# One float32 row loaded by two queues instead of one, in a batched trace of matrix products

## The chip, the core and the metric

The kernel runs on one NeuronCore of a Trainium2 chip. A core has a matrix engine (PE, with its weight loads listed apart as PEld), a vector engine (DVE), a scalar engine (ACT), a general engine (POOL) and a synchronising engine (SP). Sixteen DMA engines move data between the large memory (HBM) and the core's on-chip memory of 128 partitions. The metric is the device time of one execution in microseconds (us).

## The reference

```python
def setup_inputs():
    B, N = 8, 2176
    return {"a": np.random.randn(B, N, N).astype(np.float32),
            "b": np.random.randn(B, N, N).astype(np.float32)}

def reference(a, b):
    prod = np.matmul(a, b)
    return np.diagonal(prod, axis1=1, axis2=2).sum(axis=-1).astype(np.float32)
```

For each of eight pairs the result is the trace of A times B, which is the sum over all i and k of A[i, k] times B[k, i]. Nothing but the elementwise product of A transposed with B has to be formed, so the kernel reads 16 matrices of 2176 x 2176 float32 (303 MB) and does little arithmetic on each number.

## The kernel before

A matrix has 17 blocks of 128 rows. They are held as three groups: two of six blocks (the tiles `a_six` and `b_six` hold both, twelve blocks) and one of five (the tile `five`). Within a group of m blocks, partition p holds the m neighbouring rows m\*p to m\*p+m-1, so that each partition reads one contiguous stretch of HBM. All of these tiles are bfloat16, and the loads of them are issued by POOL (`fetch`, line 178); these loads convert from float32 on the way. They all go through one queue, called q0 on the page, and are carried out in the order of issue.

For every pair n the steps are: PE transposes blocks of A into PSUM (lines 241 and 244), ACT and DVE copy the transposed blocks into the tile `at` (lines 283 and 307), and DVE multiplies `at` with B and sums the products (line 296). A pair starts with the group of five; then follow the two groups of six. The tile `five` is shared by A and B: it is filled with A's last five blocks, transposed, and filled with B's last five blocks as soon as PE has read it (POOL waits for the semaphore `made`). For the last pair, B comes in nine pieces, of which the last ones are small, and PE forms a part of the products as 128 x 128 matmuls (line 270). Two of the small loads there have 8 partitions and one has 112, and they lie in `five` too.

The first pair is loaded in a way of its own. Of A's group of five, block 0 (the first row of each partition's five) comes by a load that ACT issues (line 153). It brings 128 partitions of 2176 float32, 8,704 bytes each, with no conversion, into `words`, which is the memory of the first two blocks of `b_six` seen as float32. ACT casts the left half of it into `five[:, 0]` (line 154), DVE the right half (line 155). Blocks 1 to 4 come by POOL's first `fetch`, and `a_six` by its second. All of that stands ahead of the hand-synchronised section (`tile_critical`) or at its beginning. On entry to the section every engine but POOL waits for the two casts. POOL issues its first two fetches before it does that (`tc.wait_critical_data_deps()`).

Then DVE writes `ones` and zeros two tiles (line 293), POOL turns these into identities (line 201), and PE starts once the identities are there and SP has seen the first fetch land (line 226: SP counts the arrivals and passes them on to PE).

SP has no loads before the change. Its one DMA is the store of the eight results at the end (line 352).

Of the kernel before, what the change touches and what calls it, by code (L numbers as in the profile page):

```python
# [21 lines left out]
def kernel(  # L22
# [6 lines left out]
    nc = tc.nc  # L29
    P = 128  # L30
# [3 lines left out]
    SIX, FIVE = 6, 5  # L34
    TWICE = 2 * SIX
# [74 lines left out]
    def flat(t):  # L110
        return t.rearrange("p r k -> p (r k)")
# [4 lines left out]
    def rows_of(src, start, m, r0, r1):  # L116
        return src[start:start + P * m, :].rearrange("(p r) k -> p (r k)", r=m)[:, r0 * N:r1 * N]
# [4 lines left out]
    def last_b(v):  # L122
        if v < TWICE:
            return b_six[:, v, :]
        return five[:, v - TWICE, :]
# [24 lines left out]


    words, middle = flat(b_six[:, 0:2, :].bitcast(f32)), N // 2
    nc.scalar.dma_start(out=words, in_=rows_of(a[0], TWICE * P, FIVE, 0, 1))
    nc.scalar.copy(out=five[:, 0, :middle], in_=words[:, :middle])
    nc.vector.tensor_copy(out=five[:, 0, middle:], in_=words[:, middle:])  # L155

    with tc.tile_critical(no_gpsimd_drain=True) as section:
# [24 lines left out]
        for n in range(BATCH):  # L182
# [14 lines left out]
            if n == 0:  # L197
                tc.wait_critical_data_deps()
                gp.wait_ge(zeros.sem, 2)
                for t in (identity32, identity16):  # L200
                    ready.by(gp.affine_select(
                        out=t, in_=t, compare_op=mybir.AluOpType.not_equal, fill=1.0, base=0,
# [49 lines left out]
        for k, (piece, (lo, hi, more)) in enumerate(zip(pieces, shares)):  # L252
            mine = []
            for v in range(piece.v0, piece.v1):
                row = last_b(v)
# [45 lines left out]
        for n in range(BATCH):  # L301
# [21 lines left out]
            out=result[:1, 0:LAST],  # L323
            in_=total[:, 0:2 * LAST].rearrange("o (b n) -> o b n", n=2),
# [18 lines left out]
        for c in range(cols):  # L343
# [9 lines left out]
            out=out.rearrange("(a b) -> a b", a=1), in_=result[:1, :],  # L353
# [40 lines left out]
```

## Time and profile before

| what | value |
|---|---|
| median of 3 runs | 707.49 us (707.47 to 707.51) |
| the profiled execution's own time | 707.37 us |
| its span, first to last instruction | 705.6 us |
| POOL's loads, queue q0 | 150.96 MB written on chip, 99.8% of 16 engines' span |
| ACT's load, queue q10 | 1.11 MB in 144 packets, 0.5% |
| HBM read | 303.04 MB, 429 GB/s over the span |
| DVE, PE, ACT, POOL busy | 54%, 28%, 29%, 4% |

The 1.8 us between the span and the execution's time lie before the first instruction or after the last one. A share of a DMA queue is the time that its packets took, summed and set against 16 engines for the whole span. The trace keeps a record of each packet with its start, its length and its queue. For a load of 128 partitions there is one data packet for each partition and a 4-byte one on each of the 16 engines that reports that it is done; so the 144 packets of q10 are 128 and 16.

### The profile page before, as it was taken

What the parts mean: (1) busy time and instruction counts of PE and PEld (TensorE: products, weight loads), DVE (VectorE), ACT (ScalarE), POOL (GpSimd) and SP (SyncE); (2) the same over time, 40 slices, a digit from 0 to 9 for tenths busy, and PEclk for the clock granted to TensorE, in tenths of its full rate; (3) what the DMA queues carried; (4) which work ended last, traced back from release to release, by engine and by line L of the source; (5) the groups of instructions that cost most, each with busy time, mean ns of one, the idle gap of its engine ahead of it and who ended that gap; (6) DMA issues with size and microseconds to landing.
All of it is one profiled execution on the core that took longest, in us unless ns stands there. A gap on an engine that the chain in (4) does not pass through costs nothing. (4 is left out here: it accounts for less than half of the span.)

```text
span 705.6 us, 3919 instructions
## 1 busy us (share of the span) xinstructions
PE 200.1 (28%) x1611; PEld 180.0 (26%) x1613; DVE 381.1 (54%) x94; ACT 204.5 (29%) x162; POOL 26.1 (4%) x48
## 2 busy tenths in 40 slices
PE   0335003450134501344012440134301343014606
PEld 0224002440124401243012430124301343014504
DVE  0105488154871549715397163961639616395478
ACT  1427002470023700346003460044500445005800
POOL 1000000000000000000000000000000000002000
PEclk9759555695557955678555785567755578556957
DMA  9999999999999999999999999999999999999998
GB/s 237 213 216 208 229 207 215 216 225 213 223 220 212 211 221 216 215 214 226 209 218 227 211 210 225 215 213 214 228 206 217 226 211 214 224 217 213 215 212 160
DMA packets 7751, 152.14 MB, mean 216 GB/s; under 512 B 706, under 2 KB 962, under 8 KB 1346
## 3 DMA queue, kind: packets, MB, share of 16 engines
q0 software_dynamic: 7600, 150.96, 99.8%
q10 hardware_dynamic: 144, 1.11, 0.5%
q8 instruction: 2, 0.03, 0.0%
q14 instruction: 3, 0.02, 0.0%
q1 hardware_dynamic: 2, 0.00, 0.0%
HBM read 303.04 MB, written 0.00 MB: 429 GB/s over the span
## 5 line engine op out<-in xcount | busy, mean ns | idle before, releaser
L283 ACT COPY at<-aT 128x1536 bf16<-128x1536 bf16 (+3 forms) x160 | 202.1, 1362 | 460.0 <-DVE sums L296 357.5
L296 DVE CUSTOM_DVE_ANT_0 at<-at,b_six 128x26112 bf16<-128x26112 bf16 (+2 forms) x9 | 214.4, 23832 | 88.8 <-DMA b_six<-in_b_dram 88.8
L307 DVE COPY at<-aT 128x1536 bf16<-128x1536 bf16 (+1 forms) x48 | 80.1, 1668 | 209.3 <-PE aT L241 158.2
L241 PE MATMUL aT<-identity,five 128*128 128x128 f32 x240 | 54.0, 412 | 369.6 <-PEq L238 369.6
L241 PEld LDWEIGHTS aT<-identity,five 128*128 128x128 f32 x240 | 46.2, 220 | 375.7 <-issue 375.7
L241 PE MATMUL aT<-identity,a_six 128*128 128x128 f32 x576 | 88.4, 313 | 99.0 <-PEq L238 98.9
L241 PEld LDWEIGHTS aT<-identity,a_six 128*128 128x128 f32 x576 | 81.2, 204 | 105.4 <-issue 105.4
L296 DVE CUSTOM_DVE_ANT_0 at<-at,five 128x10880 bf16<-128x10880 bf16 (+3 forms) x10 | 84.9, 8504 | 15.2 <-ACT at L283 14.3
L244 PE MATMUL aT<-identity,a_six 128*128 128x128 bf16 x480 | 33.5, 219 | 11.0 <-PEq L238 10.9
L244 PEld LDWEIGHTS aT<-identity,a_six 128*128 128x128 bf16 x480 | 29.5, 118 | 14.4 <-issue 14.4
L178 POOL DMA_DIRECT2D five<-in_b_dram x15 | 8.2, 553 | 290.1 <-PE aT L244 290.1
L244 PE MATMUL aT<-identity,five 128*128 128x128 bf16 x200 | 15.9, 249 | 0.0
L244 PEld LDWEIGHTS aT<-identity,five 128*128 128x128 bf16 x200 | 15.7, 128 | 0.5
L178 POOL DMA_DIRECT2D five<-in_a_dram x8 | 4.6, 577 | 294.5 <-DVE sums L296 293.7
L270 PE MATMUL trace_ps<-b_six,at 128*128 128x128 bf16 x34 | 3.8, 310 | 22.1 <-DMA b_six<-in_b_dram 22.1
L270 PEld LDWEIGHTS trace_ps<-b_six,at 128*128 128x128 bf16 x34 | 3.5, 145 | 22.2 <-issue 22.2
L178 POOL DMA_DIRECT2D b_six<-in_b_dram x10 | 6.6, 663 | 37.7 <-DVE sums L296 37.7
L178 POOL DMA_DIRECT2D a_six<-in_a_dram x9 | 6.1, 680 | 0.0
L272 PE MATMUL aT<-at 128*128 128x512 bf16 x13 | 4.1, 453 | 0.3 <-issue 0.2
L270 PE MATMUL trace_ps<-five,at 128*128 128x128 bf16 x54 | 3.8, 220 | 1.3 <-DMA five<-in_b_dram 1.3
L155 DVE CAST five<-b_six 128x1088 bf16<-128x1088 f32 x1 | 0.7, 727 | 5.8 <-DMA b_six<-in_a_dram 5.8
L270 PEld LDWEIGHTS trace_ps<-five,at 128*128 128x128 bf16 x54 | 3.1, 98 | 2.8 <-DMA five<-in_b_dram 2.4
(19 smaller groups left out, 8.7 us busy)
## 6 DMA issues: line engine op xcount, KB each, us to landing
a_six<-in_a_dram POOLq DMA_DIRECT2D x7, 6528.0 KB, 54.7
b_six<-in_b_dram POOLq DMA_DIRECT2D x7, 6528.0 KB, 52.3
five<-in_b_dram POOLq DMA_DIRECT2D x7, 2720.0 KB, 22.0
five<-in_a_dram POOLq DMA_DIRECT2D x7, 2720.0 KB, 24.4
a_six<-in_a_dram POOLq DMA_DIRECT2D x2, 3264.0 KB, 46.8
b_six<-in_b_dram POOLq DMA_DIRECT2D x1, 3264.0 KB, 31.4
five<-in_a_dram POOLq DMA_DIRECT2D x1, 2176.0 KB, 14.8
b_six<-in_b_dram POOLq DMA_DIRECT2D x1, 2176.0 KB, 41.2
```

The lines of the kernel that those rows point to most:

```text
L155: nc.vector.tensor_copy(out=five[:, 0, middle:], in_=words[:, middle:])
L178: reached = count.by(gp.dma_start(out=dst, in_=src), 16)
L241: last = pe.transpose(ps[:, place, :], src, identity32)
L244: last = pe.transpose(ps16[:, place * P:(place + 1) * P], src, identity16)
L270: ins = pe.matmul(trace_ps, x, y, start=w is real[0], stop=w is real[-1])
L272: pe.matmul(slots[0][:, 0:4, :], x, y, start=True, stop=True)
L283: ins = act.copy(out=dst, in_=view(slots[t % SLOTS]))
L296: return dve.tensor_tensor_reduce(out=x if out is None else out, in0=x, in1=y, scale=1.0, scalar=0.0, op0=MUL, op1=ADD, accum_out=acc,)
L307: ins = dve.tensor_copy(out=dst, in_=view(slots[t % SLOTS]))
```

## The change

The load of the float32 row is split by partitions. ACT issues the load of the first 16 partitions, and SP issues one for the other 112. Bytes, source, destination and the two casts stay as they are. The casts need both loads now.

```diff
     words, middle = flat(b_six[:, 0:2, :].bitcast(f32)), N // 2
-    nc.scalar.dma_start(out=words, in_=rows_of(a[0], TWICE * P, FIVE, 0, 1))
+    row, ENGINES = rows_of(a[0], TWICE * P, FIVE, 0, 1), 16
+    nc.scalar.dma_start(out=words[:ENGINES], in_=row[:ENGINES])
+    nc.sync.dma_start(out=words[ENGINES:], in_=row[ENGINES:])
     nc.scalar.copy(out=five[:, 0, :middle], in_=words[:, :middle])
     nc.vector.tensor_copy(out=five[:, 0, middle:], in_=words[:, middle:])
```

## The prediction

> **What bounds the kernel now.** I read the page's DMA row and queues first, then the chain that ended last, then the first microseconds as a timeline, and last the same stretch cut into windows.
>
> ```profile
> DMA  9999999999999999999999999999999999999998
> ...
> q0 software_dynamic: 7600, 150.96, 99.8%
> q10 hardware_dynamic: 144, 1.11, 0.5%
> ```
>
> The sixteen DMA engines are busy in every slice, and POOL's queue q0 alone fills 99.8% of their time. No compute engine is above 54%. The end of the chain of waits, in order of time (start, length, what), says the same:
>
> ```profile
> 649.44 3.04 POOL five L178 x6
> ...
> 652.61 49.60 DMA five<-in_b_dram
> 702.21 0.05 issue
> 702.26 0.63 PE trace_ps L270 x6
> ```
>
> The last load was issued at 652.61 and landed at 702.21, behind 50 us of queued transfers; 3.4 us of arithmetic and of the store follow. So the time is: when the engines begin to move data, plus their packets, plus what they idle, plus this tail. Now the start:
>
> ```profile
> 0.74 0.37 ACTq L153 DMA_DIRECT2D b_six<-in_a_dram  x1
> ...
> 1.24 0.67 POOL L178 DMA_DIRECT2D five<-in_a_dram  x1 [0.79 <-POOLq L378]
> 1.90 0.75 POOL L178 DMA_DIRECT2D a_six<-in_a_dram  x1
> 5.80 1.10 ACT L154 CAST five<-b_six 128x1088 bf16<-128x1088 f32 x1 [3.37 <-DMA b_six<-in_a_dram]
> 5.80 0.73 DVE L155 CAST five<-b_six 128x1088 bf16<-128x1088 f32 x1 [5.80 <-DMA b_six<-in_a_dram]
> ...
> 16.33 4.67 PE L241 MATMUL aT<-identity,five 128*128 128x128 f32 x25 [16.33 <-PEq L238]
> ...
> 23.93 0.56 POOL L178 DMA_DIRECT2D five<-in_b_dram  x1 [15.70 <-PE aT L244]
> ```
>
> ACT issues the row at 0.74, the casts begin at 5.80, and PE begins only at 16.33, when blocks 1 to 4 have landed. In windows (stretch, its length, busy time of five engines, clock, DMA share, GB/s; a packet counts where it starts, so a share can exceed 1):
>
> ```profile
> 1.00:1.50 0.50, 0.00 (x0) 0.00 (x0) 0.00 (x0) 0.36 (x1) 0.27 (x1) 1.00 0.00 0
> 1.50:1.75 0.25, 0.00 (x0) 0.00 (x0) 0.00 (x0) 0.25 (x1) 0.25 (x1) 1.00 0.23 35
> 1.75:2.00 0.25, 0.00 (x0) 0.00 (x0) 0.00 (x0) 0.25 (x1) 0.25 (x2) 1.00 2.49 383
> ...
> 20.00:640.00 620.00, 165.68 (x1308) 150.85 (x1306) 339.54 (x69) 174.66 (x139) 18.15 (x29) 0.63 1.01 217
> ```
>
> Nothing moves before 1.50; the first packet starts at 1.75, 1.01 us after ACT's issue. From then on no engine idles: from 20 to 640 us the share is 1.01.
>
> **The row before, in packets.** Each engine takes eight data packets (128 over 16). A packet's median in the records is 0.328 us, so 8 x 0.328 = 2.62 us at full rate. q10's packets sum to 3.26 us for each engine: the first ones, at the start of traffic, take 0.7 to 1.15. q0's first packets start from 4.90 to 5.42, on each engine within 10 ns of q10's last one, though POOL's instruction for them ended at 1.90. So q0 was ready by 4.90 at the latest, and no engine paused at the changeover.
>
> **Part 1, the issue.** ACT issues 16 rows instead of 128, and SP 112. SP leaves the same opening barrier as ACT (both have a 17 ns semaphore instruction at 0.7), so both issue at about 0.74; SP has no other work before 6.9. What a load of a few descriptors needs is bounded by the nearest rows: 128 rows took 1.01 us from issue to first packet, the store at the end, with one descriptor, 0.74 (issued at 703.66, its packet recorded at 704.41). So the first packet moves by 0 to -0.27; 16 descriptors are nearer to one than to 128, and I take -0.2.
>
> **Part 2, the packets.** One row for each engine by ACT's queue and seven by SP's is again eight for each. Sixteen more completion packets are one for each engine, 9 ns as recorded for q10: +0.01. The second load opens a stream of its own. At worst its first packets pay the slow beginning once more: 3.26 - 2.62 = +0.64. At best both beginnings run together and half of it is saved: -0.3. Since both loads are issued within tenths of a us and q0 took over from q10 without a pause, I take 0.
>
> **Part 3, sixteen neighbouring partitions.** The first 16 packets all write partitions 0 to 15, which no large load here does. The nearest row is the two 8-partition loads of the last pair (34 KB each): packets of that size (4,352 bytes) take 0.342 in the median and 0.455 at most, so crowding shows at most 0.11. A float32 packet writes twice the bytes at the same length, so I allow the double on top of its 0.328, up to +0.3, with +0.1 as the value; 0 is the other end. [...]
>
> **Part 4, the casts' wait.** Both casts now need two loads. Behind ACT's cast is nothing until 17.68; behind DVE's are three memsets (7.17 to 7.5), POOL's identities (7.70 to about 9) and with them PE's start. That chain has 16.33 - 9 = 7 us of cover. One more semaphore wait is tens of ns (17 to 21 ns a semaphore instruction): nothing. Were the cover used up, PE, then `made`, then POOL's next fetch (23.93) would be late. That fetch queues behind `a_six`, issued at 1.90 and, by the median of its size, 54.7 us in landing, so it may come 56.6 - 23.9 = 32 us later before an engine idles.
>
> **The stagger.** The engines enter q0 over a spread of 0.52 us (4.90 to 5.42), and the last engine sets the end. A new order can move the last one by about half of that: 0.3 to either side, 0 taken.
>
> **Sum.** -0.2 + 0.01 + 0 + 0.1 + 0 = -0.1 us. The profiled execution would go from 707.37 to 707.27. It stands 0.12 under the median of the runs, so the forecast for the median is 707.4. Ends: -0.27 - 0.3 - 0.3 = -0.9 (706.6) and 0 + 0.64 + 0.3 + 0.01 + 0.3 = +1.25 (708.7).
>
> **The rivals.** *Interleaving.* q0 gets onto the engines between ACT's packet and SP's seven. Its first load is eight packets of 1.30 for each engine, 10.4 us, so the row lands near 5.4 + 10.4 = 15.8 instead of 5.4, the casts and identities end near 16 + 3.2 = 19.2, and PE starts about 3 us late. For it: q0 may be ready any time after 1.90. Against: q0 never got between q10's packets. The work is only reordered, and 3 us is far inside the 32: 707.4 as well, with PE's start as its mark. [...]
>
> *Slower: the second load starts late.* If SP's load moves only once ACT's has landed (its writes kept apart, or the two queues served in turn), the row's fixed cost comes twice. That cost is 5.0 us from issue to landing less 2.62 of packets, 2.4. ACT's 16 rows would land at 0.74 + 2.4 + 0.33 = 3.5, SP's first packet would come 1.01 later at 4.5, and the engines, done with ACT's packet near 1.6 + 1.0 = 2.6, would stand idle for up to 1.9 us: 707.49 + 1.9 = 709.4. It decides only if q0 is not ready either; measurably slower (over 0.2%, 1.4 us, about what a measurement of this kernel can tell from no change) from readiness at 2.6 + 1.4 = 4.0 on. For it: readiness is known only to lie between 1.90 and 4.90. Against: two halves of `five` were written at once by the two casts, so disjoint writes are not put in order.
>
> *Slower: uneven spread.* If 112 rows went to 14 engines, these would have nine packets instead of eight: +0.33. If ACT's 16 rows went to four engines: seven and four make eleven, three more, +0.98. On two engines: fifteen, +2.3, or 709.8. All later loads are spread evenly, so an engine that enters q0 late ends late; it is measurable from five extra packets (5 x 0.328 = 1.6). Against: 16 and 112 both divide by 16.
>
> *Nothing happens*, if the engines get the same 128 packets at the same times (first packet still at 1.75): 707.5. For it: issue takes ACT 0.37 us for 128 rows and SP 0.31 for one, so little of the 1.01 goes with the number of rows.
>
> *Much faster* would need over 1.4 us. All that lies between ACT's issue and the first packet is 1.01, and the slow beginning 0.64; both would have to vanish almost wholly.
>
> **How the numbers follow.** The forecast 0.55, interleaving 0.2, nothing 0.1, a late second load 0.06 (half of it measurable), uneven spread 0.05 (half), other causes that I don't see 0.04. Measurably slower: 0.03 + 0.025, and most of the unseen, with some for the terms' upper ends together: 0.1. Faster: 0.02. Within 0.2%: 0.88. The range is the sum's ends drawn in to 706.8 below, as three best cases at once are unlikely, and left at 708.7 above.
>
> **What would show it.** First packet near 1.55 us, in the window 1.50 to 1.75; q10 with 32 packets and SP's queue with 128 (and the store's two); casts near 5.8 or, with interleaving, near 16; q0 still at 99.8%; last landing within a us of 702.2. An empty DMA window between 2.5 and 5 would show a late second load; a last landing over 703.5 with the start unchanged would speak for uneven spread. A change beyond 1.4 us would prove me wrong.

## The result and the profile after

The changed kernel takes 708.65 us in the median of 18 runs (708.37 to 709.41), the kernel before 707.55 in 18 runs beside it (707.32 to 708.06). The ratio is 1.0015 with a 95% interval of 1.0008 to 1.0022: 1.1 us slower. The profiled execution took 708.76 us with a span of 707.0, 1.4 more than before. Timed again later beside three other kernels it took 709.01 against 707.32, ratio 1.0024 (1.0014 to 1.0033).

First the queues of the changed kernel (packets, MB, share of 16 engines' span):

```profile
DMA  9999999999999999999999999999999999999997
...
q0 software_dynamic: 7600, 150.96, 99.6%
q1 hardware_dynamic: 130, 0.97, 0.6%
q10 hardware_dynamic: 32, 0.14, 0.1%
```

q1 is SP's queue: 112 data packets, 16 that report, and the store's two. The row has kept its bytes, 1.11 MB, but its share has gone from 0.5% to 0.6 and 0.1. The end of the changed kernel's chain of waits:

```profile
651.06 3.04 POOL five L180 x6
...
654.24 49.45 DMA five<-in_b_dram
703.68 0.05 issue
703.73 0.61 PE trace_ps L272 x6
```

The last landing has moved from 702.21 to 703.68, by 1.47; behind it nothing has changed. The start as a timeline:

```profile
0.74 0.41 ACTq L154 DMA_DIRECT2D b_six<-in_a_dram  x1
0.74 0.39 SPq L155 DMA_DIRECT2D b_six<-in_a_dram  x1
1.24 0.67 POOL L180 DMA_DIRECT2D five<-in_a_dram  x1 [0.79 <-POOLq L380]
...
7.70 1.28 ACT L156 ACT_TABLE_LOAD   x1 [7.70 <-DMA b_six<-in_a_dram]
7.72 0.73 DVE L157 CAST five<-b_six 128x1088 bf16<-128x1088 f32 x1 [7.72 <-DMA b_six<-in_a_dram]
8.99 1.10 ACT L156 CAST five<-b_six 128x1088 bf16<-128x1088 f32 x1
...
17.75 5.78 PE L243 MATMUL aT<-identity,five 128*128 128x128 f32 x30 [17.75 <-PEq L240]
```

Both loads are issued at 0.74, at the same time, as expected. DVE's cast comes 1.92 later than before, ACT's 3.19 and PE 1.42. And in windows, before (the prediction shows the one from 1.75 to 2.00, with 383 GB/s):

```profile
3.00:5.00 2.00, 0.00 (x0) 0.00 (x0) 0.00 (x0) 0.00 (x0) 0.00 (x0) 1.00 1.08 427
```

and after:

```profile
1.50:1.75 0.25, 0.00 (x0) 0.00 (x0) 0.00 (x0) 0.00 (x0) 0.25 (x1) 1.00 0.00 0
1.75:2.00 0.25, 0.00 (x0) 0.00 (x0) 0.00 (x0) 0.00 (x0) 0.25 (x2) 1.00 2.59 383
...
3.00:5.00 2.00, 0.00 (x0) 0.00 (x0) 0.00 (x0) 0.00 (x0) 0.00 (x0) 1.00 1.04 257
```

This is the reading that matters. Traffic begins where it began, and from 3 to 5 us the engines are as busy as before (1.04 against 1.08), but they move 257 GB/s instead of 427. Nothing idles; each packet takes longer. The packet records say how much. The 128 packets of the row had a median of 0.328 us; now the 112 have 0.51. By half microseconds their median is 0.71 and 0.65 from 3 to 4 us, and 0.44 to 0.52 from 4 us on. The row's packets sum to 4.57 us an engine (4.11 on q1, 0.46 on q10) instead of 3.26. So the engines enter POOL's queue q0 at 6.14 to 6.85 instead of 4.90 to 5.42, the last one 1.43 later, and everything behind keeps that delay to the end. (The records do not name the engine. An entry here is the start of one of q0's first 16 packets; where q0 comes after the whole row, each of them starts within 9 ns of the end of a packet of the row.)

### The profile page after: what moved, and what is told of

It is laid out like the page before. It is cut to its first block, busy times and chain, and to the rows that moved or that the text cites. A ratio compares the mean times of both kernels' runs of the same rounds, so it can differ in the third digit from the quotient of the medians.

```text
span 707.0 us, 3924 instructions
## 1 busy us (share of the span) xinstructions
PE 202.4 (29%) x1613; PEld 182.5 (26%) x1613; DVE 381.2 (54%) x94; ACT 204.8 (29%) x162; POOL 26.1 (4%) x48
## 5 line engine op out<-in xcount | busy, mean ns | idle before, releaser
L243 PEld LDWEIGHTS aT<-identity,a_six 128*128 128x128 f32 x576 | 83.1, 205 | 102.8 <-issue 102.7
```

Source lines behind the costliest of these rows:

```text
L243: last = pe.transpose(ps[:, place, :], src, identity32)
```

## The experiments

Why do the same 8,704 bytes take half as long again? Theory M: the way the rows of 112 partitions are dealt to the engines makes them hinder one another. Theory Q: two queues that work at once cost each engine time for every packet. Theory S: SP's queue is the slower one. In every edit the first lines of the diff are the changed kernel's.

**One queue (e1_one_queue).**

```diff
-    nc.scalar.dma_start(out=words[:ENGINES], in_=row[:ENGINES])
+    nc.sync.dma_start(out=words[:ENGINES], in_=row[:ENGINES])
     nc.sync.dma_start(out=words[ENGINES:], in_=row[ENGINES:])
```

> The same two loads, 16 and 112 rows, but both issued by SP on one queue. Theory M (the way 112 rows are dealt to the 16 engines, seven neighbouring partitions each, makes them hinder one another): the 112 rows' packets stay at 0.42 to 0.52 us after the start, the last engine enters POOL's queue q0 near 6.8 us, time as in the changed kernel, 708.4 to 709.2. Theory Q (two queues at once cost each engine time for every packet): packets back at 0.33, last engine enters q0 near 5.4 to 5.8, time 707.3 to 708.0.

Measured: 708.14 us (707.97 to 709.03, 10 runs) against 707.51, ratio 1.0008 (0.9999 to 1.0018). The packets stay long, 0.42 to 0.51 after 3 us, and the last engine enters q0 at 6.45. The long packets speak for M. But the time is below the 708.4 that M had named, and its interval reaches no change; that it is a little faster than the change is taken up by the last experiments.

**The whole row by SP (e2_whole_sp).**

```diff
-    nc.scalar.dma_start(out=words[:ENGINES], in_=row[:ENGINES])
-    nc.sync.dma_start(out=words[ENGINES:], in_=row[ENGINES:])
+    nc.sync.dma_start(out=words, in_=row)
```

> All 128 rows in one load, issued by SP instead of ACT. Theory S (SP's queue is the slower one): packets 0.42 to 0.52, last engine enters q0 near 6.8, 708.4 to 709.2. Theories M and Q: as before the change, packets 0.33, q0 near 5.4, 707.3 to 708.0.

Measured: 707.37 (707.26 to 707.48, 10 runs), ratio 0.9996 (0.9986 to 1.0005); packets 0.328, last entry 5.44. S falls.

**Two queues, split by columns (e3_columns).**

```diff
-    nc.scalar.dma_start(out=words[:ENGINES], in_=row[:ENGINES])
-    nc.sync.dma_start(out=words[ENGINES:], in_=row[ENGINES:])
+    part = N // 8
+    nc.scalar.dma_start(out=words[:, :part], in_=row[:, :part])
+    nc.sync.dma_start(out=words[:, part:], in_=row[:, part:])
```

> Two queues as in the change, split by columns: ACT brings the first 272 of 2176 float32 of all 128 partitions, SP the other 1904. Theory M: each load is dealt as 128 rows are, so packets of 7,616 bytes take 0.29, the last engine enters q0 near 5.4 to 6.0 (128 more packets of 1,088 bytes), 707.3 to 708.2. Theory Q: packets stay stretched by about half, 0.4 or more, q0 near 6.5 or later, 708.4 or more.

Measured: 707.31 (707.25 to 707.57, 10 runs), ratio 0.9995 (0.9985 to 1.0005). The packets of 7,616 bytes take 0.288, the last entry is at 5.49. The bytes are shared between the queues as in the change, and the loss is gone. Q falls as the main cause: what hurts is the split by partitions.

**Halves of neighbours (e4_halves) and halves of every second partition (e12_halves_strided).** The second was run later; the two belong together.

```diff
-    nc.scalar.dma_start(out=words[:ENGINES], in_=row[:ENGINES])
-    nc.sync.dma_start(out=words[ENGINES:], in_=row[ENGINES:])
+    nc.scalar.dma_start(out=words[:64], in_=row[:64])        # e12: words[0::2], row[0::2]
+    nc.sync.dma_start(out=words[64:], in_=row[64:])          # e12: words[1::2], row[1::2]
```

> Two queues, 64 partitions each, four rows for each engine from each. Theory M: dealt as four neighbours for an engine, rows 0 to 63 together and 64 to 127 together; packets between 0.33 and 0.66, the last engine enters q0 between 5.4 and 7.5, depending on which neighbours hinder one another. Theory Q: stretched as in the change, 0.42 to 0.52, q0 near 6.8.

> Two loads of 64 partitions as in the run with halves, but ACT takes the even partitions and SP the odd ones, so that each load reaches over all 128. [...] If the number of rows dealt to an engine (four) is what matters: 0.66 and 7.7, 709.3, as with halves.

Windows of the halves of neighbours:

```profile
4.00:5.00 1.00, 0.00 (x0) 0.00 (x0) 0.00 (x0) 0.00 (x0) 0.00 (x0) 1.00 0.87 183
5.00:6.00 1.00, 0.00 (x0) 0.00 (x0) 0.00 (x0) 0.00 (x0) 0.00 (x0) 1.00 1.10 252
```

and of the halves of every second partition:

```profile
4.00:5.00 1.00, 0.00 (x0) 0.00 (x0) 0.00 (x0) 0.19 (x1) 0.00 (x0) 1.00 0.97 409
5.00:6.00 1.00, 0.00 (x0) 0.00 (x0) 0.00 (x0) 1.00 (x1) 0.00 (x0) 1.00 1.64 418
```

Two loads, two queues and 64 rows each in both kernels, and both send their first packet at 2.06; only which partitions (and the source rows that belong to them) go together differs. Neighbours: packets of 0.66 in the median, twice 0.328, last entry into q0 at 7.70 (I had allowed 7.5), 709.34. Every second one: 0.33, last entry 5.69, 707.61 (one run each, beside 707.51 and 707.37). This is the strongest evidence for M: the packet doubles and returns to 0.33 with nothing changed but which partitions, and their source rows, go together. Which engine carries which partition is in no record of this trace, so that neighbours are dealt to one engine is M's assumption and not shown.

**Write side or read side: eight loads of 16 (e5_sixteens, e6_spread, e7_crossed).** Theory W: the hindrance lies where the packets are written. Theory R: in the source rows that are read at one time, since the split by partitions changes these too.

```diff
-    nc.scalar.dma_start(out=words[:ENGINES], in_=row[:ENGINES])
-    nc.sync.dma_start(out=words[ENGINES:], in_=row[ENGINES:])
+    for p in range(0, P, ENGINES):                            # e5
+        nc.scalar.dma_start(out=words[p:p + ENGINES], in_=row[p:p + ENGINES])
+    for p in range(8):                                        # e6
+        nc.scalar.dma_start(out=words[p::8], in_=row[p::8])
+    for p in range(8):                                        # e7
+        nc.scalar.dma_start(out=words[ENGINES * p:ENGINES * (p + 1)], in_=row[p::8])
```

> The row as eight loads of 16 neighbouring partitions, all by ACT: each engine still gets eight packets, one of each load. [...] Theory R (it is on the read side, from which source rows are read at one time): nothing about the destination matters, so it is told by the next two runs, of which this one should then differ from both in the same way. If 16 neighbours cost nothing: packets 0.33, q0 entered within the pace of ACT's eight issues, near 5.5 to 6.5.

> Eight loads of 16 partitions again, but each takes every eighth partition (and the source rows that belong to them). Theory W: packets shorter than in the run with 16 neighbours, by about half of its excess over 0.33, and q0 entered sooner. Theory R: longer or shorter, and equal to the crossed run.

> Eight loads of 16 neighbouring destination partitions, but filled from every eighth source row; the rows so land in other partitions than the second matrix's, and the first result is of another sum. Theory W: like the run with 16 neighbours (packets and entry into q0 within 10%). Theory R: like the run with every eighth partition.

Measured, one run each, beside 707.27: 709.75, 708.31, 709.43. The row's data packets sum to 3.80, 2.88 and 3.63 us an engine. The crossed run has the destination of the first and the source of the second, and it behaves like the first, within 5%: W. From the third load on, away from the start of traffic, the packets take 0.43, 0.34 and 0.40 in the mean, the same picture. One thing weakens it: ACT took 5.09 us to issue the eight loads of the spread run, against 4.14 and 3.96, so a part of its ease may be that fewer of its packets met. The price was less than I had estimated (the packets' median in the first run is 0.39, where I looked for 0.5 or more, and the time 709.75, where I looked for 710 or more), and the mark "last entry into q0" is of no use here: q0 gets in between the eight loads from 2.6 to 2.8 us on, and part of the loss is in q0's own packets (those of 17,408 bytes rise from 1.30 to 1.39 in the mean in e5, 1.38 in e7 and 1.35 in e6).

**Other source rows (e8_other_rows).** The split as changed, with source rows that lie one behind the other.

```diff
-    nc.scalar.dma_start(out=words[:ENGINES], in_=row[:ENGINES])
-    nc.sync.dma_start(out=words[ENGINES:], in_=row[ENGINES:])
+    nc.scalar.dma_start(out=words[:ENGINES], in_=a[1, :ENGINES, :])
+    nc.sync.dma_start(out=words[ENGINES:], in_=a[1, ENGINES:P, :])
```

> The changed kernel with 16 and 112 partitions as it has them, but the source is the first 128 rows of the second matrix, one behind the other (8,704 bytes apart instead of 43,520); the first result is of another sum. Theory W: packets of the 112 rows stay at 0.42 to 0.52, q0 entered by the last engine near 6.8. Theory R: they change, most likely to 0.33 with q0 near 5.5.

Measured: 709.06 in one run; packets 0.39 to 0.50 from 4.5 us on, but 0.83 to 0.98 from 3 to 4.5, and the last entry 7.14 instead of 6.85. Moving the source has not helped, as W has it; what makes the packets before 4.5 us longer still than in the change is open.

**112 rows first (e9_112_first).**

```diff
-    nc.scalar.dma_start(out=words[:ENGINES], in_=row[:ENGINES])
     nc.sync.dma_start(out=words[ENGINES:], in_=row[ENGINES:])
+    nc.sync.dma_start(out=words[:ENGINES], in_=row[:ENGINES])
```

> Both loads by SP on one queue, 112 rows first and the 16 rows behind them, so that the 16 neighbours come when traffic is under way. [...] Last engine enters q0 at 6.2 to 7.2.

Measured: 708.39 in one run, first entry into q0 at 5.63, last at 6.64. The price of the 16 rows, which come when traffic is under way, can't be read off: q0 came in ahead of them on some engines (its longest packet is 1.77 instead of 1.30), so the last packets of the row, 0.62 in the median from 5.5 us on, hold that as well. Inconclusive for what it was meant for.

**No row at all (e10_no_row).** POOL brings all five blocks.

```diff
-    nc.scalar.dma_start(out=words[:ENGINES], in_=row[:ENGINES])
...
-    nc.vector.tensor_copy(out=five[:, 0, middle:], in_=words[:, middle:])
...
-                fetch(d_a5, flat(five[:, 1:FIVE, :]), rows_of(a[0], TWICE * P, FIVE, 1, FIVE), 1)
+                fetch(d_a5, flat(five), rows_of(a[0], TWICE * P, FIVE, 0, FIVE), 1)
```

> No float32 row: POOL's first fetch brings all five blocks with conversion, and the two casts fall away. It shows when q0 can start by itself. If q0 is ready when POOL's instruction has ended, its first packet comes at 2 to 3 us, and the time is 707.5 to 708.8 (the start is later than 1.75 by that much, less what the row's slow first packets cost). If it needs longer, up to 4.90, the time is up to 710.5.

Measured: 708.38 (708.26 to 708.79, 10 runs) against 707.47, ratio 1.0012 (1.0002 to 1.0021). q0's first packet comes at 2.61, 0.86 later than ACT's at 1.75, and the time is 0.91 longer. So ACT's row buys just about the time in which POOL's queue isn't ready, and the changed kernel, 1.1 slower than the kernel before, gives all of that back. Whether it is even slower than having no such row isn't shown: the intervals of the two ratios overlap.

**Why the change is slower than one queue (e11_swapped, then r1 to r4 on one chip).**

```diff
-    nc.scalar.dma_start(out=words[:ENGINES], in_=row[:ENGINES])
-    nc.sync.dma_start(out=words[ENGINES:], in_=row[ENGINES:])
+    nc.sync.dma_start(out=words[:ENGINES], in_=row[:ENGINES])
+    nc.scalar.dma_start(out=words[ENGINES:], in_=row[ENGINES:])
```

> The change with the queues swapped: SP brings the 16 rows, ACT the 112. The changed kernel was 0.5 us slower than the same two loads on one queue with the 16 first. Theory O (what counts is the order in which the two loads get onto the engines; in the changed kernel SP's first packets came at 1.75 and ACT's at 2.42 though both were issued at 0.74): now the 16 rows come first, and the time is that of the run on one queue, 707.9 to 708.3, last engine into q0 near 6.4. Theory Q2 (two queues cost 0.5 us beside the dealing): as the change, 708.4 to 708.9, q0 near 6.8.

Measured: 708.43 (707.95 to 708.70, 10 runs), ratio 1.0012 (1.0002 to 1.0021), last entry 6.58: the time is at the edge of Q2's range, the entry between the two theories. The four again with more runs; r1 is the change, r2 is e1, r3 is e11, r4 is e2:

> The changed kernel again, beside the next three on one chip. Theory M alone (the dealing of the rows is the whole loss): within 0.2 us of the run on one queue. Theory Q2 (two queues add to it): 0.4 to 0.6 above the run on one queue, and the swapped one close to this. Theory O (the order of the two loads adds to it): 0.4 to 0.6 above the run on one queue, and the swapped one close to that.

> 16 and 112 rows, both by SP: 708.0 to 708.3, as its first time; the last engine enters q0 at 6.3 to 6.6 us.

> SP 16 rows, ACT 112. Theory O: 708.0 to 708.3. Theory Q2: 708.5 to 708.8. Its first time, 708.43, lay between.

> All 128 rows by SP. If the issuing engine makes no difference, as theory M has it: the kernel before within 0.1 us. Its first ten runs lay from 707.26 to 707.48, while runs of the kernel before fall into two groups, 707.2 to 707.6 and 707.9 to 708.3; if that is more than chance, this one's median is 0.1 to 0.4 lower.

| kernel | median of 11 runs | range | ratio to before (707.32, 33 runs) |
|---|---|---|---|
| the change | 709.01 | 708.63 to 709.34 | 1.0024 (1.0014 to 1.0033) |
| one queue, 16 first | 708.57 | 707.99 to 708.70 | 1.0014 (1.0005 to 1.0024) |
| queues swapped, 16 first | 708.50 | 708.23 to 709.32 | 1.0017 (1.0007 to 1.0026) |
| whole row by SP | 707.32 | 707.22 to 707.88 | 1.0000 (0.9991 to 1.0009) |

Two queues with the 16 rows first equal one queue with the 16 first, 708.50 and 708.57, though both are above the 708.0 to 708.3 that I had named. So two queues as such add nothing that shows; the change alone, in which SP's 112 start at 1.75 and ACT's 16 at 2.42, is 0.44 to 0.51 above them. The traces show where: in both traces of the change the 112's packets that start from 3 to 4 us take 0.65 to 0.72 in the median of each half microsecond, in both of the swapped kernel 0.48 to 0.55, and in both of the one queue 0.35 to 0.44. That the order makes it fits theory O, but the intervals overlap and no run shows how, so this part stays open. For the whole row the engine that issues makes no difference: SP's median equals that of the kernel before, and the lower one that its first ten runs had suggested did not come.

The row's packets and the end go together over the kernels in which q0 starts after the whole row (both kernels with 64 partitions a load begin 0.31 later, at 2.06):

| kernel | row's packets, us an engine | last entry into q0 | end of q0's last packet |
|---|---|---|---|
| before | 3.26 | 5.42 | 702.2 |
| whole row by SP | 3.28 | 5.44 | 702.3 |
| columns | 3.32 | 5.49 | 702.4 |
| every second partition | 3.22 | 5.69 | 702.5 |
| one queue, 16 and 112 | 4.08 | 6.45 | 703.1 |
| swapped | 4.33 | 6.58 | 703.3 |
| the change | 4.57 | 6.85 | 703.7 |
| other source rows | 4.76 | 7.14 | 704.0 |
| halves of neighbours | 5.06 | 7.70 | 704.3 |

The second traces of four of them show how well one trace repeats: the change 4.67 and 7.05, one queue 3.85 and 6.07 (an entry before the 6.3 that I had named), swapped 4.44 and 6.71, whole row by SP 3.16 and 5.43.

## Why the prediction was wrong

The time lies in the range, at its upper edge, but the forecast was 0.1 faster and the kernel is 1.1 slower. That the range holds it is luck: its upper end was made of a second slow beginning, a crowding of the 16 rows and the stagger, and none of these is where most of the time went.

**What failed is part 2, the packets.** It priced eight packets an engine at what a load of 128 partitions pays, looked only for a second slow beginning (0, at worst +0.64), and never asked whether a packet of a load of 112 partitions costs what a packet of a load of 128 costs. Parts 2 and 3 together measured +1.31 (4.57 against 3.26). About 0.1 of that is the sixteen rows', so part 2 comes to about +1.2, nearly twice its upper end. The halves of neighbours against every second partition, and the crossed loads, show that the partitions written together set it (packets of 0.66 against 0.33; 3.80 and 3.63 us an engine against 2.88).

**Part 1, the issue,** took -0.2 and got 0: the first packet is at 1.75 as before, and it is SP's. The 16 rows began later, at 2.42. The store's 0.74 was the wrong row to lean towards.

**Part 3, sixteen neighbours,** looked for a crowding of neighbours and put it on the wrong load: the 112's packets rose from 0.328 to 0.51. The 16 rows' data packets took 0.44 in the mean instead of 0.328, the +0.1 of the sum. But its row, two small loads with conversion, writes half the bytes in the same time, and so said little of crowding. Besides, the 0.342 and 0.455 were taken over all 256 packets of 4,352 bytes, and only 16 of these belong to the two small loads; 112 belong to the last pair's load of 112 partitions and 128 to one of all 128, and all but two of the 256 took 0.341 to 0.345. So the nearest row for 112 partitions gave no warning either. Why neighbours cost more than partitions that lie apart no run shows.

**Part 4, the casts' wait,** held: DVE's cast came 1.92 later, and PE's start, 1.42 later, moved only with the fetch that lands behind the row. One thing was missing: before, ACT loaded its table (1.28) under the wait; in the changed kernel it waits first, and so its cast comes at 8.99. The identities had also ended at 8.24 before the change, not near 9, so the cover was 8.1 us and not 7. It was large enough.

**The stagger** went from 0.52 to 0.71, 0.16 of the last engine's 1.43 (in the second trace of the change it was 1.14).

**The rivals.** Interleaving did not come: q0 was ready from 2.61 (the kernel without the row) and still started on each engine only after both loads. A late second load fell with it: both loads moved near the beginning, at 1.75 and 2.42, and with q0 ready at 2.6 its condition, readiness from 4.0 on, was not met. Uneven spread: the sign named for it came, a last landing over 703.5 with the start unchanged, but it misled, for the last engine entered q0 only 0.7 after the first, so no few engines carried the excess. The point that held best was that of the opening paragraphs: the end follows the engines' entry into q0 one for one (in the change 1.47 and 1.43 later).

## What to carry to other kernels

A load split by partitions was not the same load here: the price of a packet of 8,704 bytes depended on which partitions were written at the same time, 0.33 us for all 128 or for every second one, 0.51 for 112 neighbours beside the other 16, 0.66 for 64 neighbours. Where a load must be shared between queues, try the split by columns first: here it took 707.31 us beside 707.51, the split by partitions 708.65 beside 707.55. And DMA engines that were equally busy didn't move the same: from 3 to 5 us a share of 1.08 went with 427 GB/s before and one of 1.04 with 257 after. So set the bytes beside the share, in windows of the stage.

## What the runs showed of the hardware

POOL's queue, whose first packet came at 2.61 us in the run without the row, did not get between the eight packets that an engine had from one load of ACT or SP (before: entry at 4.90 to 5.42), nor between the two loads of the change; it did get between eight loads on one queue, so that DVE's cast in the run with eight loads of neighbours came at 25.04, and on some engines ahead of the 16 rows in the run with 112 first. In the run with halves of neighbours the loads of both queues ran one after the other, SP's to 5.14 and ACT's from 4.30 on; in the run with columns they ran side by side, ACT's from 1.76 to 4.63 and SP's from 1.91 to 5.49. Which rule decides between the two is open.

The first issue took 0.53 to 0.56 us for 64 partitions, where it took 0.37 to 0.41 for 16 neighbours, 112 or 128, and the first packet came at 2.06 instead of 1.75, in both runs with halves. In the spread run, 16 partitions that reach over all 128 took 0.58, and the first packet came at 2.10. The run with every second partition:

```profile
0.74 0.55 ACTq L154 DMA_DIRECT2D b_six<-in_a_dram  x1
0.74 0.53 SPq L155 DMA_DIRECT2D b_six<-in_a_dram  x1
...
6.08 0.73 DVE L157 CAST five<-b_six 128x1088 bf16<-128x1088 f32 x1 [6.08 <-DMA b_six<-in_a_dram]
```

Why 64 partitions cost more to issue than 112 is open.
